# A decoder step in retention and cross attention: the samples' q and k rows reach all partitions by DMA through DRAM, not by selector products

## The chip, the cores and the metric

The kernel runs on one core of one Trainium2 chip. The metric is the device time of one execution in microseconds, the median of several runs. The work is float32 throughout; products of large matrices are made from two float32r halves of each operand (a high part `wh`, `B[0]`, `A[0]` and a low part `wl`, `B[1]`, `A[1]`), three products for one.

## The reference, cut to what matters

Two layers, each `x += mixer(norm(x)); x += cross_attention(norm(x)); x += conv_ffn(norm(x))`, for a prompt of 256 positions and for 8 samples of one new position each, with the same weights. Layer 0 mixes by retention; the change touches only the samples in it:

```python
q, k, v, g = jnp.split(h @ w_in, [nqk, 2 * nqk, 2 * nqk + nv], axis=-1)
q = rotary(q.reshape(B, L, RET_HEADS, RET_DK).astype(F32), offset)
k = rotary(k.reshape(B, L, RET_HEADS, RET_DK).astype(F32), offset) * (RET_DK ** -0.5)
...
o = att(q, k, v) + jnp.einsum('bihd,bhde->bihe', q * q_dec, s)   # reads the state
s = s * chunk_dec + jnp.einsum('bjhd,bjhe->bhde', k * k_dec, v)  # writes the new state
```

With one position a sample needs, for each of 4 heads, its old state (256 x 512) times its q row, and the new state, gamma times the old one plus the outer product of its k row and its v row.

## The kernel before

**Main stream.** `run` goes through a list of units in order. A unit is a tile of 128 output features: its weights come in chunks of 128 x 1024 (512 KB) into one of 6 raw slots (`wraw`), are split by ACT into `wh` and by DVE into `wl` (4 slots each), and TensorE makes three products of 264 columns for each step of 128 rows of the contraction (8 steps to a chunk). The order of the weights: retention in (48 chunks, with the prompt's memory keys and values of layer 0 among them), retention out (`ret_w_out`, 16 chunks, of which 9 come before `K.ret_done`), cross attention, FFN, then layer 1 in the same way.

**Everything else** is a task, a Python generator that issues some instructions and yields. `Clock` is a rough model of the engines' queues, the DMA among them; the task whose due time comes first goes next, and prefetches start when the model's DMA is not too far ahead and when the arena `ar` has room (`prefetch`, `reserve`). So the order of all instructions on all engines is fixed when the program is built, and any change of a cost, a wait or of the arena's size moves it. All loads and stores are issued by one queue, SP's, in order; DVE, ACT and TensorE are queues in order too.

**The samples of a head.** A state lies as 128 partitions x 4 x 256, the 256 of the head's q or k dimension along the free axis. So the q row must be there on every partition. `ret_qk` transposes q and k of the 8 samples to rows, and writes each as two float32r halves (partitions 0 to 7 and 32 to 39) into `rget` storage in `f` (q) and into `kst` (k). `bcast` then multiplies a column of the selector `sel` (40 partitions, given to TensorE 128 times over) by these 40 rows: two products of 256 columns put two samples' rows on all partitions of a PSUM bank. `settle` copies the bank to SBUF (128 x 512, ACT). `ret_samples` uses that for four `scalar_tensor_tensor` with `accum_out` for each state (`junkt<-kvt,x`), `ret_update`, which runs beside the two FFNs, for four `scalar_tensor_tensor` that make the new state (`kvt<-x,vst,kvt`). A pair of rows serves two states; there are 16 pairs for q and 16 for k.

**After the samples** of a head come `ret_norm` (a norm over the head's output of prompt and samples: products with a column of ones, Newton steps on DVE, three small products that spread the factors, an ACT copy, two DVE products of 128 x 528) and `ret_fin`, which makes the head's four tiles of `B`: for each a DVE product, an ACT cast for the high half, a DVE subtraction for the low half. `K.ret_done` holds the main stream until that is done for all four heads; the tenth chunk of `ret_w_out` is the first that reads tiles 12 to 15 of `B`, head 3's.

Of the kernel before, what the change touches and what calls it, by code (L numbers as in the profile page):

```python
# [56 lines left out]
C_ID, C_ONE, C_COS, C_SIN, C_MASK = 0, P, 2 * P, 2 * P + NT, 2 * P + 3 * NT  # L57
C_DEC = C_MASK + H * T
C_SEL = C_DEC + 2 * H
C_SUM = C_SEL + S  # L60
# [7 lines left out]
def _constants():  # L68
    half = D // H // 2
    inv = np.float32(10000.0) ** (-np.arange(half, dtype=np.float32) / np.float32(half))  # L70
    pos = np.concatenate([np.arange(T), np.full(S, PAST)]).astype(np.float32)
    ang = (inv[:, None] * pos[None, :]).astype(np.float32).astype(np.float64)
    c = np.zeros((P, NCST), np.float64)
    c[:, C_ID:C_ID + P] = np.eye(P)
    c[:, C_ONE:C_ONE + P] = 1.0
    c[:, C_COS:C_COS + NT] = np.cos(ang)
    c[:, C_SIN:C_SIN + NT] = np.sin(ang)
    c[:, C_SIN + NT:C_SIN + 2 * NT] = np.cos(ang)
    j = np.arange(P)[:, None]
    i = np.arange(T)[None, :]  # L80
    for h in range(H):
        rel = i - j
        m = np.where(rel >= 0, _gamma(h) ** np.maximum(rel, 0), 0.0) / 16.0
        c[:, C_MASK + h * T:C_MASK + (h + 1) * T] = m
        for t in range(2):
            c[:, C_DEC + 2 * h + t] = _gamma(h) ** (T - 1 - t * P - np.arange(P)) / 16.0
    for s in range(S):
        c[[s, LO + s], C_SEL + s] = 1.0
        c[LO * (s % 4) + s, C_SUM + s] = 1.0
    return c.astype(np.float32)  # L90
# [80 lines left out]
class Clock:  # L171
    """A rough model of the engines' queues, by which the order of the instructions is chosen."""
# [79 lines left out]
class Kern:  # L252
# [188 lines left out]
    def split_at(self):  # L441
        """When the next chunk of the stream can be split, as far as that is known."""
# [7 lines left out]
    def calm(self, n):  # L450
        """When chunk n of the stream, which is not the next to be used, may get in the way of other work."""
# [28 lines left out]
    def need(self, c):  # L480
        """Chunk c is the next of the stream to be used."""
# [164 lines left out]
    def proj(self, src, src_rhs, evac, n=NT, parts=False, tag=None):  # L646
        """The chunks in src hold the rows of one 128-feature tile, in order; with parts a unit each."""
# [31 lines left out]
    def pair(a, b, cut=6):  # L679
        """Two projections of one chunk each, with the last rows of the contraction of both at the end."""  # L680
# [24 lines left out]
    def newton(self, a, y, n, root=False):  # L705
        """y = a ** -0.5: a first guess from the exponent bits, or the root from a table, then Newton steps."""
# [14 lines left out]
    def rsqrt_mean(self, sq, n, cnt, wide=False, tok=None, root=False):  # L721
        """[128, n] copies of (column sums of sq / cnt + EPS) ** -0.5; a generator that returns them."""
# [42 lines left out]
    def norm_later(self, wide=False):  # L765
        """The factors of the norm over what self.sq holds, as self.r, a few steps on."""
# [190 lines left out]
    def ret_qk(self, h):  # L957
# [37 lines left out]
    def rget(self, n):  # L995
        b = self.rarena.get(n)
        while b is None:
            yield WAIT
            b = self.rarena.get(n)
        return b  # L1000
# [73 lines left out]
    def ret_samples(self, h):  # L1074
        hd = self.hd[h]
        while "qk" not in hd["flags"]:
            yield WAIT
        yield from self.lock("s")
        qr = hd["qr"].ap
        acc = self.get(4 * S)  # L1080
        av = acc.v(4, S)
        nb = yield from self.bcast(qr, 0)
        yield WAIT
        nxt = yield from self.settle(nb)
        for pr in range(4):
            cur = nxt
            if pr < 3:
                nb = yield from self.bcast(qr, 2 * pr + 2)
            else:
                hd["qr"].free()  # L1090
# [10 lines left out]
            if pr < 3:  # L1101
                nxt = yield from self.settle(nb)
# [18 lines left out]
    def ret_update(self, heads):  # L1121
        """New retention states of the samples: gamma * state + k v^T."""
# [3 lines left out]
        nb = yield from self.bcast(self.kst[:, order[0][0], :], order[0][1])  # L1126
        t0 = self.now
        for n, (h, s) in enumerate(order):
            if s % 2 == 0:
                yield WAIT  # L1130
# [72 lines left out]
    def residual(self, gain, scale=False):  # L1203
        """What becomes of the sums of output tile m: they are added to x."""
# [49 lines left out]
    def blocks(self, plan, rows, evac):  # L1254
        """A unit for each (chunk, tiles, k): the chunk holds rows k, ... of the contraction for some output tiles."""
# [60 lines left out]
    def parts(self, src, dims):  # L1316
        """A copy of src in two parts of fewer bits that add up to it."""
# [74 lines left out]
    def bcast(self, src, n0):  # L1392
        """Two rows of src, n0 and n0 + 1, on all partitions of a bank."""
        b = yield from self.wbank()
        for s2 in range(2):
            self.mm(self.ps[:, b, s2 * 256:(s2 + 1) * 256], self.sel[:, n0 + s2:n0 + s2 + 1].to_broadcast([LO + S, P]),
                    src[:LO + S, :256], True, True)
        return b
# [25 lines left out]
    def gather(self, b, rows):  # L1424
        """Column s of half t of bank b: row 32 (s % 4) + s of columns 128 t to 128 t + 127 of rows."""
# [136 lines left out]
    def lru_prep(self):  # L1562
        # 8 log_sigmoid(lam) = 8 (min(lam, 0) - log1p(exp(-|lam|))), log1p(z) = 2 artanh(z / (2 + z))
# [22 lines left out]
    def lru(self):  # L1586
# [3 lines left out]
        def half(name, m, n=4):  # L1590
            """Feature tile m of a buffer that is kept for half of the tiles."""
# [154 lines left out]
# How eager each part of the program is, in us: patience (2), slack of the task kinds 1 to 3, tilt, ahead.  # L1746
# [7 lines left out]
def tile_hybrid_step(ctx: ExitStack, tc: tile.TileContext, ins, outs):  # L1754
# [12 lines left out]
    K.sel = pool.tile([LO + S, S], F32R, name="sel")  # L1767
# [14 lines left out]
    K.kst = pool.tile([P, H, 256], F32R, name="kst")  # L1782
# [7 lines left out]
    nc.vector.memset(kvt[:, 0, :1024], 0.0)  # L1790
    nc.vector.tensor_copy(K.kst.rearrange("p a b -> p (a b)"), kvt[:, 0, :1024])
# [3 lines left out]
    ROOM = 28160 + 1024 * (6 - K.NR) - 128 - 128 - S - 2 * 2 * KD * M  # L1795

    def enter(nb, maxpre, reserve, slots, main):
        def go():
# [11 lines left out]
            if nb == 16:  # L1810
                K.rarena = Arena(ft, 512)
                nc.vector.tensor_copy(ft[:, :512], kvt[:, 0, :512])
# [88 lines left out]
    def staged(units, n):  # L1901
        """The last part of each of the first n tiles comes after the other parts of all of them."""
# [6 lines left out]
    items += [tune(12, 7200, (1,), 4), lambda: K.cp(K.sel, K.cst[:LO + S, C_SEL:C_SEL + S]),  # L1909
              lambda: K.add(K.mem_norm(0), 1)] + qkv[0][6:]  # L1910
# [3 lines left out]
    def out(w, plan, rows, gain):  # L1914
        """plan: what to wait for, or chunks of w."""
# [132 lines left out]
```

## Time and profile before

| | |
|---|---|
| median of 3 runs | 1046.58 us (1046.05 to 1047.74) |
| span of the profiled execution, first to last instruction | 1044.7 us |
| what the median of the runs has beyond that span | 1.9 us |
| TensorE busy | 1023.0 us (98%) |
| VectorE (DVE) busy | 807.4 us (77%) |
| ScalarE (ACT) busy | 589.4 us (56%) |
| DMA, mean | 245 GB/s |

The profiled execution's own time is its span; no other time of it is shown, so the rest of a run is taken as 1.9 us throughout. Times in the rows are us from the span's start. A matmul's duration covers its way through the array, and the next starts before it ends, so what a product costs a full TensorE is read from the starts of the rows, not from durations. In a merged row of several instructions the time runs from the first start to the last end.

### The profile page before, as it was taken

The numbers are of one execution on the slowest core, as the hardware profiler recorded it, in microseconds if no ns is written. First come the engines' busy times: TensorE is split into PE (matmuls) and PEld (weight loads), VectorE is DVE, ScalarE is ACT, GpSimd is POOL, SyncE is SP. The second block draws the span as 40 slices with busy tenths as digits, with TensorE's granted clock in tenths as the row PEclk, the third lists the DMA queues.
The fourth block names the chain that finished last, engine by engine and source line by source line (L and its number), as shares of the span: only waits on it lengthen the run. The fifth ranks groups of instructions, "written<-read, shape, count | busy, mean of one in ns | idle before, by whom it ended". The sixth has DMA issues, their size and how long they took to land.

```text
span 1044.7 us, 20974 instructions
## 1 busy us (share of the span) xinstructions
PE 1023.0 (98%) x8158; PEld 966.4 (93%) x8158; DVE 807.4 (77%) x1685; ACT 589.4 (56%) x979; POOL 84.4 (8%) x190
## 2 busy tenths in 40 slices
PE   7999999999999999999999999999999999999996
PEld 7988999889998868999999999999878999999996
DVE  7968788777677644898988776989755898898773
ACT  6554555455545434575676554697444666766552
POOL 0000000000000000023221000400000222121000
PEclk9999999999999999999999999999999999999998
DMA  9667766774766897567888977546886668777851
GB/s 371 207 216 248 272 224 232 263 262 164 271 218 235 297 315 256 191 212 259 266 297 291 301 235 233 172 164 233 311 286 223 209 203 290 272 256 272 299 192 62
DMA packets 70916, 255.45 MB, mean 245 GB/s; under 512 B 8096, under 2 KB 8736, under 8 KB 70304
## 3 DMA queue, kind: packets, MB, share of 16 engines
q1 hardware_dynamic: 70384, 253.53, 70.4%
q8 instruction: 64, 1.05, 0.4%
q10 hardware_dynamic: 432, 0.58, 0.2%
q14 instruction: 36, 0.29, 0.1%
HBM read 229.34 MB, written 24.74 MB: 243 GB/s over the span
## 4 chain that ended last, share of the span: by engine, by line
PE 87%; DVE 6%; DMA 3%; ACT 3%; issue 1%; SPq 0%; DVEq 0%; ACTq 0%
PE ps L274 83%; PE ps L279 3%; DVE wl L293 2%; DVE x L299 2%; DVE x L293 1%; DMA kvt<-in_cache_v 1%; DMA x<-in_cache_k 1%; ACT x L329 1%; PE ps L289 1%; ACT L329 1%; ACT wh L333 1%; DMA kvt<-in_cache_k 1%; DVE x L318 0%; DMA wraw<-in_ret_w_in 0%; DVE B L293 0%
## 5 line engine op out<-in xcount | busy, mean ns | idle before, releaser
L274 PE MATMUL ps<-A,wh 128*128 128x264 f32 x2816 | 525.1, 287 | 7.1 <-ACT A L329 6.3
L333 ACT CAST wh<-wraw 128x1024 fp32r<-128x1024 f32 x284 | 297.2, 1049 | 281.3 <-PE ps L274 237.2
L274 PEld LDWEIGHTS ps<-A,wh 128*128 128x128 f32 x2816 | 437.2, 189 | 16.0 <-ACT A L329 6.3
L293 DVE TENSOR_TENSOR wl<-wraw,wh 128x1024 fp32r<-128x1024 f32 x296 | 359.2, 1220 | 93.4 <-ACT wh L333 85.6
L274 PE MATMUL ps<-A,wl 128*128 128x264 f32 x1408 | 400.1, 284 | 0.1
L274 PE MATMUL ps<-B,wh 128*128 128x264 f32 (+1 forms) x1664 | 311.8, 288 | 2.2 <-DVE B L293 2.2
L274 PEld LDWEIGHTS ps<-B,wh 128*128 128x128 f32 x1664 | 257.3, 188 | 12.7 <-issue 8.6
L274 PEld LDWEIGHTS ps<-A,wl 128*128 128x128 f32 x1408 | 265.1, 188 | 0.4 <-DVE wl L293 0.3
L274 PE MATMUL ps<-B,wl 128*128 128x264 f32 (+1 forms) x832 | 235.5, 283 | 0.0
L274 PEld LDWEIGHTS ps<-B,wl 128*128 128x128 f32 x832 | 156.2, 188 | 0.0
L293 DVE TENSOR_TENSOR x<-ps,x 128x264 f32<-128x264 f32 (+2 forms) x248 | 83.9, 364 | 33.1 <-PE ps L274 21.2
L337 POOL COPY x<-x 128x16 f32<-128x16 f32 (+2 forms) x162 | 78.3, 518 | 268.1 <-DVE x L293 217.2
L329 ACT ACTIVATE x<-x 128x264 f32<-128x264 f32 (+4 forms) x166 | 59.7, 389 | 20.2 <-DVE x L293 8.7
L299 DVE SCALAR_TENSOR_TENSOR x<-x,par 128x280 f32<-128x280 f32 (+3 forms) x128 | 61.5, 488 | 2.3
L333 ACT COPY x<-ps 128x512 f32<-128x512 f32 (+3 forms) x85 | 39.2, 475 | 42.0 <-PE ps L274 31.2
L299 DVE SCALAR_TENSOR_TENSOR kvt<-x,vst,kvt 128x256 f32<-128x256 f32 x128 | 53.3, 477 | 1.3 <-ACT kvt L329 1.3
L299 DVE SCALAR_TENSOR_TENSOR junkt<-kvt,x 128x256 bf16<-128x256 f32 x128 | 46.4, 420 | 9.1 <-DMA kvt<-in_state_ret 6.4
L293 DVE TENSOR_TENSOR x<-x 128x264 f32<-128x264 f32 (+6 forms) x106 | 44.8, 435 | 7.7 <-ACT x L329 5.8
L333 ACT CAST B<-x 128x264 fp32r<-128x264 f32 (+2 forms) x84 | 34.7, 417 | 24.5 <-DVE x L293 17.4
L329 ACT ACTIVATE x<-x,par 128x280 f32<-128x280 f32 (+2 forms) x64 | 38.6, 605 | 8.9 <-DVE x L293 5.9
L293 DVE TENSOR_TENSOR B<-x,B 128x264 fp32r<-128x264 f32 (+2 forms) x84 | 36.7, 438 | 8.4 <-ACT B L333 8.2
L274 PE MATMUL ps<-wh,B 128*128 128x512 f32 x128 | 42.5, 400 | 0.0
(100 smaller groups left out, 703.6 us busy)
## 6 DMA issues: line engine op xcount, KB each, us to landing
wraw<-in_ffn_w_up SPq DMA_DIRECT2D x96, 512.0 KB, 4.4
kvt<-in_state_ret SPq DMA_DIRECT2D x64, 512.0 KB, 6.0
wraw<-in_ret_w_in SPq DMA_DIRECT2D x48, 512.0 KB, 4.4
wraw<-in_ffn_w_down SPq DMA_DIRECT2D x48, 512.0 KB, 4.7
out_ret_s<-kvt SPq DMA_DIRECT2D x32, 512.0 KB, 5.1
x<-in_cache_v SPq DMA_DIRECT2D x18, 512.0 KB, 6.7
wraw<-in_xa_w_k SPq DMA_DIRECT2D x16, 512.0 KB, 4.4
wraw<-in_xa_w_v SPq DMA_DIRECT2D x16, 512.0 KB, 4.1
```

The lines of the kernel that those rows point to most:

```text
L274: self.last = self.nc.tensor.matmul(out, lhsT, rhs, start=start, stop=stop)
L279: self.nc.tensor.matmul(out, lhsT, rhs, start=start, stop=stop, tile_position=(0, LO * j))
L289: self.nc.tensor.transpose(out, in_, self.ident[:n, :n])
L293: self.nc.vector.tensor_tensor(out=out, in0=a, in1=b, op=op)
L299: self.nc.vector.scalar_tensor_tensor(out, a, s, b, op0, op1, **kw)
L329: self.nc.scalar.activation(out, in_, func, **kw)
L333: self.nc.scalar.copy(out, in_)
L337: self.nc.gpsimd.tensor_copy(out, in_)
```

## The change

q and k rows no longer go through TensorE and PSUM to all partitions. `ret_qk` writes plain float32 rows of q and k side by side into one buffer of 8 partitions, `ret_rows` stores it into a DRAM tile `qk` (4 heads x 2 x 8 samples x 256), and `spread` loads two samples' rows (2 KB) from there into each of 128 partitions. `bcast`, `settle`, `rget`, `sel`, `kst` and the two zero fills at the start are gone; the 1024 words of `kst` go to the arena (`ROOM`). The samples of a head wait for a flag `rows` that the model sets 1 us after the store. Comments are gone too.

```diff
-        hr = yield from self.rget(256)
-        hd["qr"] = hr
-        hv, kv = hr.ap, self.kst[:, h, :]
-        self.cp(hv[:S, :], ps[:S, :256])
-        self.act(kv[:S, :], ps[:S, 256:], AF.Copy, scale=1.0 / 16.0)
-        self.tt(hv[LO:LO + S, :], ps[:S, :256], hv[:S, :].bitcast(F32), SUB)
-        self.stt(kv[LO:LO + S, :], ps[:S, 256:], 1.0 / 16.0, kv[:S, :].bitcast(F32), MUL, SUB)
+        rows = yield from self.wget(512)
+        rv = rows.ap[:S, :512]
+        self.cp(rv[:, :256], ps[:S, :256])
+        self.act(rv[:, 256:], ps[:S, 256:], AF.Copy, scale=1.0 / 16.0)
+        self.add(self.ret_rows(h, rows))
...
+    def ret_rows(self, h, rows):
+        yield self.c.written(rows.ap[:, :512])
+        t = self.store(self.qk[h].rearrange("t s d -> s t d"), rows.ap[:S, :512].rearrange("s (t d) -> s t d", t=2))
+        yield t + 1000.0
+        rows.free()
+        self.hd[h]["flags"].add("rows")
+
+    def spread(self, h, t, s):
+        b = yield from self.wget(512)
+        while self.c.used(b.ap) > self.now + 500.0:
+            yield self.c.used(b.ap) - 400.0
+        src = self.qk[h, t, s:s + 2, :].rearrange("s d -> (s d)").partition_broadcast(P)
+        return b, self.load(b.ap[:, :512], src)
...
     def ret_samples(self, h):
-        while "qk" not in hd["flags"]:
+        while "rows" not in hd["flags"]:
             yield WAIT
...
-        nb = yield from self.bcast(qr, 0)
-        yield WAIT
-        nxt = yield from self.settle(nb)
+        nxt = yield from self.spread(h, 0, 0)
         for pr in range(4):
-            cur = nxt
+            cur, at = nxt
             if pr < 3:
-                nb = yield from self.bcast(qr, 2 * pr + 2)
-            else:
-                hd["qr"].free()
+                nxt = yield from self.spread(h, 0, 2 * pr + 2)
+            if at > self.now:
+                yield at
...
     def ret_update(self, heads):
-        nb = yield from self.bcast(self.kst[:, order[0][0], :], order[0][1])
+        nxt = yield from self.spread(*order[0][:1], 1, 0)
...
             if s % 2 == 0:
-                yield WAIT
-                kb = yield from self.settle(nb)
+                kb, at = nxt
+                if at > self.now:
+                    yield at
                 if n + 2 < len(order):
-                    nb = yield from self.bcast(self.kst[:, order[n + 2][0], :], order[n + 2][1])
+                    nxt = yield from self.spread(order[n + 2][0], 1, order[n + 2][1])
...
-    def bcast(self, src, n0):
-        b = yield from self.wbank()
-        for s2 in range(2):
-            self.mm(self.ps[:, b, s2 * 256:(s2 + 1) * 256], self.sel[:, n0 + s2:n0 + s2 + 1].to_broadcast([LO + S, P]),
-                    src[:LO + S, :256], True, True)
-        return b
-
-    def settle(self, b):
-        t = yield from self.wget(512)
-        self.cp(t.ap[:, :512], self.ps[:, b, :])
-        self.unbank(b)
-        return t
...
-    ROOM = 28160 + 1024 * (6 - K.NR) - 128 - 128 - S - 2 * 2 * KD * M
+    ROOM = 29184 + 1024 * (6 - K.NR) - 128 - 128 - S - 2 * 2 * KD * M
```

Counted over the whole program: TensorE loses the 64 selector products and nothing else; ACT loses 32 copies of 128 x 512; DVE loses 8 operations on 8 x 256 and three fills at the start; SP issues 4 stores and 32 loads more. The rest is the same work in another order. Three places show the order.

On TensorE, at the start of the update of the states beside the first FFN (`kst,sel` are the selector products), before:

```order
L274 MATMUL ps<-A,wh 128x264 x2
L274 MATMUL ps<-A,wl 128x264
L274 MATMUL ps<-kst,sel 128x256 x2
L274 MATMUL ps<-A,wh 128x264 x2
L274 MATMUL ps<-A,wl 128x264
L274 MATMUL ps<-kst,sel 128x256 x2
```

With the change, the same place:

```order
L272 MATMUL ps<-A,wh 128x264 x2
L272 MATMUL ps<-A,wl 128x264
L272 MATMUL ps<-A,wh 128x264 x2
L272 MATMUL ps<-A,wl 128x264
L272 MATMUL ps<-sq,cst 128x264
L272 MATMUL ps<-A,wh 128x264 x2
```

The pairs are gone and the main stream's products stand next to each other; `sq,cst` is the norm's product, which stands a few steps later in the program before.

On DVE, the end of head 3's norm and its four tiles of `B` (`x<-x 128x264`, then `B<-x,B`), then the weights (`wl`) up to the first sums of the output projection (`x<-ps,x`, the tenth chunk's result), before:

```order
L293 TENSOR_TENSOR x_88<-x_88 128x264
L293 TENSOR_TENSOR B_85<-x_88,B_85 128x264
L293 TENSOR_TENSOR x_88<-x_88 128x264
L293 TENSOR_TENSOR B_85<-x_88,B_85 128x264
L293 TENSOR_TENSOR wl<-wraw,wh 128x1024 x9
L293 TENSOR_TENSOR x<-ps,x 128x264 x2
```

With the change, on DVE:

```order
L291 TENSOR_TENSOR wl<-wraw,wh 128x1024 x2
L291 TENSOR_TENSOR x_86<-x_86 128x528 x2
L291 TENSOR_TENSOR x_86<-x_86 128x264
L291 TENSOR_TENSOR B_84<-x_86,B_84 128x264
L291 TENSOR_TENSOR x_86<-x_86 128x264
L291 TENSOR_TENSOR B_84<-x_86,B_84 128x264
L291 TENSOR_TENSOR x_86<-x_86 128x264
L291 TENSOR_TENSOR B_84<-x_86,B_84 128x264
L291 TENSOR_TENSOR x_86<-x_86 128x264
L291 TENSOR_TENSOR B_84<-x_86,B_84 128x264
L291 TENSOR_TENSOR wl<-wraw,wh 128x1024
L291 TENSOR_TENSOR x<-ps,x 128x264 x2
```

And on TensorE with the change, from the three small products that spread head 3's factors to the tenth chunk, whose products wait for that head's tiles one after the other:

```order
L272 MATMUL ps<-cst,x_86 128x128 [waits DVE_49]
L272 MATMUL ps<-cst,x_86 128x128
L272 MATMUL ps<-cst,x_86 128x8
...
L272 MATMUL ps<-B_84,wh 128x264 x2
L272 MATMUL ps<-B_84,wl 128x264
L272 MATMUL ps<-B_84,wh 128x264 [waits Activation_49]
L272 MATMUL ps<-B_84,wh 128x264 [waits DVE_49]
L272 MATMUL ps<-B_84,wl 128x264
L272 MATMUL ps<-B_84,wh 128x264 [waits Activation_49]
L272 MATMUL ps<-B_84,wh 128x264 [waits DVE_49]
L272 MATMUL ps<-B_84,wl 128x264
```

Five steps of the main stream stand between the small products and the first of these waits (eight rows left out). Head 3's samples moved back by some 100 steps of the main stream: before, nine chunks of weights were split between its last tile and the sums, now one is.

On SP, the loads around the end of layer 0's cross attention (`in_cache_v` are the samples' memory values), before:

```order
L350 DMA wraw<-in_xa_w_o 128x1024
L350 DMA x_88<-in_cache_v 128x1024
L350 DMA wraw<-in_xa_w_o 128x1024 x2
L350 DMA x_88<-in_cache_v 128x1024 x3
L350 DMA wraw<-in_xa_w_o 128x1024
L350 DMA x_88<-in_cache_v 128x1024
L350 DMA wraw<-in_xa_w_o 128x1024 x2
```

With the change:

```order
L348 DMA x_86<-in_cache_v 128x1024
L348 DMA wraw<-in_xa_w_v 128x1024
L348 DMA x_86<-in_cache_v 128x1024 x4
L348 DMA wraw<-in_xa_w_v 128x1024
L348 DMA x_86<-in_cache_v 128x1024 x3
L348 DMA wraw<-in_xa_w_o 128x1024 x2
```

The last of these loads moved from behind the sixth of the eight `xa_w_o` chunks to ahead of the first.

## Rows read from the trace of the kernel before

**Rows 1.** The page: span, and busy time of the engines.

```profile
span 1044.7 us, 20974 instructions
PE 1023.0 (98%) x8158; PEld 966.4 (93%) x8158; DVE 807.4 (77%) x1685; ACT 589.4 (56%) x979; POOL 84.4 (8%) x190
```

**Rows 2.** Windows beside the first FFN: busy us of each engine, clock, DMA.

```profile
440.00:460.00 20.00, 19.86 (x161) 19.37 (x160) 19.79 (x39) 15.07 (x24) 5.91 (x11) 1.00 0.56 178
500.00:520.00 20.00, 20.00 (x164) 19.72 (x164) 19.16 (x38) 13.69 (x23) 6.52 (x12) 1.00 0.80 258
```

**Rows 3.** Timeline of PE: start, us, then the products; a selector pair.

```profile
431.69 0.28 PE L274 MATMUL ps<-A,wl 128*128 128x264 f32 x1
...
432.06 0.28 PE L274 MATMUL ps<-A,wl 128*128 128x264 f32 x1
432.27 0.50 PE L274 MATMUL ps<-kst,sel 40*128 40x256 f32 x2
432.69 0.51 PE L274 MATMUL ps<-A,wh 128*128 128x264 f32 x2
433.04 0.28 PE L274 MATMUL ps<-A,wl 128*128 128x264 f32 x1
```

**Rows 4.** Timeline of PE: a pair next to other small products.

```profile
92.16 0.50 PE L274 MATMUL ps<-f,sel 40*128 40x256 f32 x2
92.59 0.83 PE L274 MATMUL ps<-cst,x 128*128 128x1 f32 x6
```

**Rows 5.** Groups by form: what is removed.

```profile
L333 ACT COPY x<-ps 128x512 f32<-128x512 f32 x48 | 27.6, 582 | 17.6 <-PE ps L274 13.8 <-DVE junkt L299 3.0 <-ACT kvt L333 0.5
...
L274 PE MATMUL ps<-f,sel 40*128 40x256 f32 x32 | 8.0, 329 | 0.0
L274 PE MATMUL ps<-kst,sel 40*128 40x256 f32 x32 | 8.0, 329 | 0.0
```

**Rows 6.** Timeline of all engines: head 3's norm, first tiles of `B`.

```profile
235.74 0.51 PE L274 MATMUL ps<-cst,x 128*128 128x128 f32 x4
...
236.28 0.38 ACT L333 COPY x<-ps 128x264 f32<-128x264 f32 x1 [1.05 <-PE ps L274]
...
236.69 1.32 DVE L293 TENSOR_TENSOR x<-x 128x528 f32<-128x528 f32 x2
...
239.98 0.43 DVE L293 TENSOR_TENSOR x<-x 128x264 f32<-128x264 f32 x1
240.44 0.41 ACT L333 CAST B<-x 128x264 fp32r<-128x264 f32 x1 [1.31 <-DVE x L293]
240.88 0.43 DVE L293 TENSOR_TENSOR B<-x,B 128x264 fp32r<-128x264 f32 x1 [0.48 <-ACT B L333]
241.24 0.42 DVE L293 TENSOR_TENSOR x<-x 128x264 f32<-128x264 f32 x1
```

**Rows 7.** Timeline: the output projection starts on PE; head 3's last tile.

```profile
249.23 0.40 PE L274 MATMUL ps<-B,wh 128*128 128x264 f32 x2
...
256.26 0.43 DVE L293 TENSOR_TENSOR B<-x,B 128x264 fp32r<-128x264 f32 x1 [0.49 <-ACT B L333]
```

**Rows 8.** Windows, columns as in rows 2: where TensorE has gaps.

```profile
368.00:372.00 4.00, 3.46 (x30) 2.85 (x28) 2.75 (x7) 0.76 (x2) 0.00 (x0) 1.00 0.95 246
372.00:376.00 4.00, 3.16 (x29) 2.52 (x30) 0.56 (x1) 1.40 (x3) 0.00 (x0) 1.00 0.89 348
712.00:716.00 4.00, 2.70 (x23) 2.49 (x21) 3.97 (x6) 1.84 (x3) 0.90 (x2) 1.00 0.54 177
...
1036.00:1040.00 4.00, 1.45 (x6) 1.35 (x6) 1.98 (x6) 0.38 (x1) 0.00 (x0) 0.50 0.02 7
```

**Rows 9.** DMA issues: count, KB each, median us from issue to landing.

```profile
kvt<-in_state_ret SPq DMA_DIRECT2D x64, 512.0 KB, 6.0
...
out_ret_p<-x SPq DMA_DIRECT2D x8, 256.0 KB, 5.8
```

**Rows 10.** Waits: engine, tile, line, released by; us in total, times, longest.

```profile
DVE junkt L299 <- DMA kvt<-in_state_ret: 6.4, 4, 3.3
...
SPq L350 <- DVE wl L293: 516.7, 196, 10.8
```

More of the change, by code (lines that the diff above doesn't have):

```diff
@@ L58 @@
 C_DEC = C_MASK + H * T
-C_SEL = C_DEC + 2 * H
-C_SUM = C_SEL + S
+C_SUM = C_DEC + 2 * H
 NCST = C_SUM + S
@@ L87, in _constants @@
     for s in range(S):
-        c[[s, LO + s], C_SEL + s] = 1.0
         c[LO * (s % 4) + s, C_SUM + s] = 1.0
@@ L993, in ret_qk @@
         hd["flags"].add("qk")
-    def rget(self, n):
-        b = self.rarena.get(n)
-        while b is None:
-            yield WAIT
-            b = self.rarena.get(n)
-        return b
+    def ret_rows(self, h, rows):
[10 more added lines that the diff above has]
+        return b, self.load(b.ap[:, :512], src)
     def ret_attn(self, h):
@@ L1075, in ret_samples @@
         hd = self.hd[h]
-        while "qk" not in hd["flags"]:
+        while "rows" not in hd["flags"]:
             yield WAIT
         yield from self.lock("s")
-        qr = hd["qr"].ap
         acc = self.get(4 * S)
         av = acc.v(4, S)
-        nb = yield from self.bcast(qr, 0)
-        yield WAIT
-        nxt = yield from self.settle(nb)
+        nxt = yield from self.spread(h, 0, 0)
         for pr in range(4):
-            cur = nxt
+            cur, at = nxt
             if pr < 3:
-                nb = yield from self.bcast(qr, 2 * pr + 2)
-            else:
-                hd["qr"].free()
+                nxt = yield from self.spread(h, 0, 2 * pr + 2)
+            if at > self.now:
+                yield at
             for s2 in range(2):
@@ L1100, in ret_samples @@
             cur.free()
-            if pr < 3:
-                nxt = yield from self.settle(nb)
         while "attn" not in hd["flags"]:
@@ L1129, in ret_update @@
             if s % 2 == 0:
-                yield WAIT
-                kb = yield from self.settle(nb)
+                kb, at = nxt
+                if at > self.now:
+                    yield at
                 if n + 2 < len(order):
-                    nb = yield from self.bcast(self.kst[:, order[n + 2][0], :], order[n + 2][1])
+                    nxt = yield from self.spread(order[n + 2][0], 1, order[n + 2][1])
             st = yield from self.take(("up", h, s))
@@ L1390, in xa_prompt @@
         xh["flags"].add("prompt")
-    def bcast(self, src, n0):
-        b = yield from self.wbank()
-        for s2 in range(2):
-            self.mm(self.ps[:, b, s2 * 256:(s2 + 1) * 256], self.sel[:, n0 + s2:n0 + s2 + 1].to_broadcast([LO + S, P]),
-                    src[:LO + S, :256], True, True)
-        return b
-    def settle(self, b):
-        t = yield from self.wget(512)
-        self.cp(t.ap[:, :512], self.ps[:, b, :])
-        self.unbank(b)
-        return t
     def samples(self, b, w, kind, l, h):
@@ L1766, in tile_hybrid_step @@
     K.par = pool.tile([P, NPRM], F32, name="par")
-    K.sel = pool.tile([LO + S, S], F32R, name="sel")
+    K.qk = ctx.enter_context(tc.tile_pool(name="rows", bufs=1, space=bass.MemoryType.DRAM)).tile([H, 2, S, 256], F32, name="qk")
     K.junkt = pool.tile([P, 2, 256], BF16, name="junkt")
@@ L1781, in tile_hybrid_step @@
     K.rfree, K.hfree = deque(range(K.NR)), deque(range(K.NH))
-    K.kst = pool.tile([P, H, 256], F32R, name="kst")
     K.vst = pool.tile([P, H, 4, S], F32, name="vst")
@@ L1789, in tile_hybrid_step @@
     K.r0 = None
-    nc.vector.memset(kvt[:, 0, :1024], 0.0)
-    nc.vector.tensor_copy(K.kst.rearrange("p a b -> p (a b)"), kvt[:, 0, :1024])
     box = []
     FR = 3072
-    ROOM = 28160 + 1024 * (6 - K.NR) - 128 - 128 - S - 2 * 2 * KD * M
+    ROOM = 29184 + 1024 * (6 - K.NR) - 128 - 128 - S - 2 * 2 * KD * M
     def enter(nb, maxpre, reserve, slots, main):
@@ L1810, in go @@
             if nb == 16:
-                K.rarena = Arena(ft, 512)
-                nc.vector.tensor_copy(ft[:, :512], kvt[:, 0, :512])
                 K.mn = (bt[:, 0, 8:, :M], bt[:, 1, 8:, :M])
@@ L1908, in tile_hybrid_step @@
     items = [policy(0), enter(16, 0, 7200, (1,), 7), start, K.pair(*qkv[0][:2], 4), want_mem] + qkv[0][2:6]
-    items += [tune(12, 7200, (1,), 4), lambda: K.cp(K.sel, K.cst[:LO + S, C_SEL:C_SEL + S]),
-              lambda: K.add(K.mem_norm(0), 1)] + qkv[0][6:]
+    items += [tune(12, 7200, (1,), 4), lambda: K.add(K.mem_norm(0), 1)] + qkv[0][6:]
     items += qkv[1] + [K.mem_sure(0)] + kv0[:4] + qkv[2] + kv0[4:6] + gs[0] + qkv[3] + kv0[6:8] + gs[1] + kv0[8:] + gs[2] + gs[3]
```

## The prediction

> **What bounds the kernel now.** I read the page first: TensorE is busy 1023.0 of 1044.7 us [rows 1], so what it issues sets the time, and the question for each edit is whether it takes products from TensorE or makes it wait. The windows over the span then show where it is full. Beside the first FFN it issues 164 products in 20 us without a gap; in the window where DVE is fullest (19.79 of 20) TensorE already misses 0.14 us [rows 2]. Gaps of any size are few: 0.54 and 0.84 us in cross attention with the DMA engines 89 to 95% busy, 1.30 us in the recurrent layer with DVE full [rows 8]. The timeline gives what a product costs a full TensorE. A step of the main stream (three products of 264 columns) runs from 431.69 to 432.06, so 0.37 us; the next step has a selector pair in it and runs from 432.06 to 433.04, so 0.98 us [rows 3].
>
> **What the change takes from TensorE.** 32 pairs of selector products. The page's 329 ns mean [rows 5] is a passage through the array, not a cost; the cost is the starts: 0.98 - 0.37 = 0.61 us for a pair in the main stream [rows 3]. Only 0.42 us of it lies between the pair and what follows; the rest is delay ahead of the pair and behind it. Of the 32 pairs in the timeline 25 stand so, alone between main products; 7 touch other small products, which would break the stream anyway, and for those I take 0.43 us [rows 4]. Sum: 25 x 0.61 + 7 x 0.43 = 15.3 + 3.0 = 18.3 us, 16 pairs in retention and 16 beside the FFNs. Bounds: 32 x 0.43 = 13.8 and 32 x 0.61 = 19.5 us.
>
> The Trainium skill, page "TensorE: Matmul & The Clock Gate", section "Back-to-back issue gap", prices a product of N columns alone at N / 2.4 + 2.5 ns when warm, so 109 ns for 256 columns, and by that figure the pairs would give 64 x 0.109 = 7.0 us, 11.3 us less than the rows. The trace does not agree for these products: the start-to-start time of a pair is 0.43, not 0.22 us [rows 4], and I go by the rows.
>
> **What it takes from the others.** 32 ACT copies of 0.58 us, 18.6 us [rows 5], and 3 us of small DVE work. ACT is at 56% and DVE at 77% [rows 1], and TensorE hardly waits for them, so I cost this at nothing. The three fills at the start lie ahead of the first weights: nothing.
>
> **What it adds.** SP issues 36 more transfers, 8 MB in all. SP's queue spends half the span waiting for a raw slot, which DVE's `wl` frees [rows 10], so issuing is free. Landing is not shown for such a load. The nearest rows: a store with the same 2 KB per partition takes 5.8 us, a state of twice the size 6.0 us [rows 9]. A head's samples now wait for two landings one after the other, some 12 us, where they waited for two products and a copy. That is no time in itself, since the main stream goes on; it counts only where the samples' end holds the stream.
>
> **Where it counts: the tenth chunk of the output projection.** Before, the projection starts at 249.23 and head 3's last tile is there at 256.26 + 0.43 = 256.7 [rows 7]; the tenth chunk starts 72 steps in, at 249.23 + 72 x 0.37 = 275.9, so 19 us of cover. With the change the order puts the small products that spread head 3's factors five steps ahead of that chunk: the cover is gone. I put the rows of before into the new order. Small products end at 235.74 + 0.51 = 236.25, five steps take 1.85, so TensorE reaches the first wait at 238.1. ACT's copy and DVE's two products of 128 x 528 end at 236.69 + 1.32 = 238.01; then come the four tiles, with nothing between them now. From a tile's start (239.98) its high half is there after 0.87 us, its low half after 1.33, and the next tile starts after 1.26 [rows 6]. The last low half is there at 238.01 + 3 x 1.26 + 1.33 = 243.1, and two products later, at 243.4, TensorE is through what it would have done by 238.1 + 4 x 0.37 = 239.6. That is a stall of 3.8 us; two splits of weights now stand ahead of the norm on DVE, and I take 4.0. Bounds: 0, if head 3 runs earlier than the planned order needs, and 7: in the stall TensorE works about a third of the time, and at 1.45 busy of 4 us the granted clock stood at 0.50, at 2.70 of 4 it stayed at 1.00 [rows 8]; at half clock for some 3 us the next steps would cost 3 us more. Nothing gives the stall back: behind it the stream is full again.
>
> **The rest of the new order.** In layer 0's cross attention the 32 loads of the samples' memory end ahead of the output weights, six chunks (17 us of stream) earlier than before. The DMA engines there are 89 to 95% busy already, and the gaps in TensorE are 1.4 us [rows 8]. Bounds: 1.4 us gained, if these gaps go; 9 us lost, if six loads of 524 KB at the 348 GB/s of that window, 1.5 us each, have to be waited for in full. I take 1.0 lost, near the rows: the same nearly full DMA costs 1.4 now. In retention DVE stands 6.4 us in four waits for states [rows 10] and TensorE has no gap there, since up to four chunks lie split ahead of it. With 16 loads of q rows on the same engine I take 1.0 us lost; the bounds are 0 and the rival below. Beside the FFNs a pair of rows is loaded two states, about 20 us, ahead: nothing.
>
> **Sum:** 1044.7 - 18.3 + 4.0 + 1.0 + 1.0 = 1032.4 us of span; with the 1.9 us that the median has beyond the span, 1034.3 us.
>
> **Rivals.**
> (a) *The stall is covered.* Head 3's samples run ahead of the plan, or ahead of the waiting products by 4 us. For it: the order is only an order, an instruction may start as soon as its inputs are there. Against: the small products are themselves in TensorE's queue, five steps ahead of the chunk. Then 1034.3 - 4.0 - 1.0 = 1029.3 us with a quiet retention.
> (b) *Transfers hold cross attention.* All 9 us of the bound: 1034.3 + 8 = 1042.3 us. For it: 95% busy DMA. Against: the bytes of the stage stay the same.
> (c) *Slower: DVE waits for q rows.* A `junkt` operation on DVE now waits for a load that was issued only one chunk of weights (2.9 us) earlier, if it lands as late as rows 9 say; behind it on DVE stand the `wl` splits, and TensorE waits for those. The longest such wait now is 3.3 us [rows 10], and it is covered. If of each of the 16 loads 2.0 us reached TensorE, that is 32 us in place of the 1.0 taken: 1065 us. It decides from 14.3 / 16 = 0.9 us for each. Against: the four split chunks are 11 us of cover.
> (d) *No change.* Two ways. The fixed part of a pair's cost stays, because DVE's splits set the pace as soon as TensorE runs freer: then a pair gives back only its stream time, 2 x 0.12 = 0.25 us (a third of a step for each product [rows 3]), 8 us in all, and 1034.3 + 10.3 = 1044.6 us. Or every stall at its bound. For it: DVE at 19.79 of 20 in one window [rows 2]. Against: over the span DVE has 237 us to spare [rows 1]. The Trainium skill's price above (same page and section) would lead to about the same time, 1045.6 us, and it has its chance within this case.
>
> On the loads of (c): the Trainium skill, page "DMA: Bandwidth & Descriptors", section "Rules for kernel authors", says that a broadcast as the outermost, short dimension confines a transfer to a few of the sixteen engines; here the outermost dimension is the 128 partitions, so by that rule all sixteen work and the load is like any other. No row shows it yet.
>
> **Chances.** The forecast 0.52, (a) 0.15, (b) 0.15, (c) 0.10, (d) 0.08. The time is that of the forecast, 1034.3, whose own range with its bounds is 1030 to 1039. The range takes in (a) and (b), from 1027 (the pairs at 19.5 us and no stall) to 1044, and leaves out (c) and (d), 0.18. A measurement of this kernel can't tell a change under 0.2% (2.1 us) from none. Faster by more: forecast, (a) and (b), 0.82; within: (d), 0.08; slower: (c), 0.10.
>
> **What the changed profile would show.** TensorE's products 64 fewer and its steps in the stretches beside the FFNs at 0.37 us without breaks; the stretches from 440 to 600 and from 820 to 1000 each about 5 us shorter. In the tenth chunk of the output projection a wait of TensorE for `B` from ACT and DVE, 3 to 5 us in four parts; if it isn't there, (a). In cross attention a wait for `in_cache_k` or `in_cache_v` of 1 to 3 us; of 5 or more, (b). In retention `junkt` waits for `x<-qk`, and TensorE stays full; if its gaps there sum to 5 us or more, (c). A landing of `x<-qk` of 4 to 7 us; far more, 20 us say, and the loads are held by the one row that they all read, which would make the prediction wrong, as would a main stream whose steps stay above 0.37 us with the pairs gone.

## The result, and the profile after

The changed kernel takes 1031.97 us (median of 4 runs, 1030.98 to 1032.11), the kernel before, on the same chip, 1046.48 us (4 runs). The ratio is 0.9847, with a 95% interval of 0.9832 to 0.9861: 1.5% or 14.5 us faster. The profiled spans are 1029.2 and 1044.7 us. One thing the count under the change leaves out: six casts of weights to their high half went from ACT (284 to 278) to DVE (12 to 18).

The page of the changed kernel, answering to [rows 1]: TensorE has 64 products and 17.0 us of work less.

```profile
span 1029.2 us, 20860 instructions
PE 1006.0 (98%) x8094; PEld 957.4 (93%) x8094; DVE 803.9 (78%) x1680; ACT 567.9 (55%) x940; POOL 83.9 (8%) x190
```

Both programs put the same 6912 products of the weight stream through TensorE in the same order. So the start of the k-th of them can be subtracted from its start before, and the difference of two such differences says what a stage gained. Worked out so from the two traces, and from those of the experiments below (us against the kernel before; minus is faster). The columns end at products 1400, 1830, 2500, 4300, 5200 and 6911; the first cut stands 13 steps ahead of the output projection, the others near the stages' ends.

```
                    retention  output   cross      FFN 0  recurrent layer,  FFN 1   sum
                               proj.    att. 0            cross att. 1
the change            -10.3    +8.1     -1.8       -5.2      -0.8           -5.0   -15.0
e1 first pair early    -9.3    +1.8     -2.2       -5.3      +0.9           -5.0   -19.2
e2 full rows           -3.6     0.0     -0.3       -3.2      -0.1           -2.9   -10.1
e3 update only         -0.5     0.0     -0.4       -5.3      +5.0           -5.0    -6.0
e4 pairs twice         +3.2     0.0     +0.8       +1.8      +0.6           +1.8    +8.6
e5 retention early    -10.7    +2.3     +0.5        0.0      +1.3            0.0    -6.2
e6 old room            -7.9    +1.8     +0.2       -5.3      +3.1           -5.0   -12.7
e7 loads twice        +11.0    +7.8     -1.1       -5.2      -0.6           -5.0    +7.3
e8 spare loads         -5.5    +7.6     -1.0       -5.2      +0.2           -5.0    -8.9
```

(Each row's sum has up to 0.4 us that arise ahead of the first product, and rounding. What lies behind the last product is in no column: it gives the span 0.5 us more in the change and 1.1 us more in e1 and e3.) In the rows of the change, e1, e5, e6, e7 and e8 three groups of head 3's small products stand behind product 1400 and not ahead of it. They move 1.8 us from the first column to the second, which is all that e1 and e6 show there. Of the change's +8.1, then, 6.3 us are a loss, and its retention gained 8.5 us and not 10.3.

Where the gain is. Windows of the changed kernel, answering to [rows 2], columns as there: the steps are unbroken, 167 and 168 products in 20 us.

```profile
440.00:460.00 20.00, 20.00 (x168) 20.00 (x167) 19.72 (x44) 14.72 (x25) 4.02 (x15) 1.00 0.66 217
500.00:520.00 20.00, 20.00 (x167) 20.00 (x167) 17.50 (x35) 13.87 (x24) 4.69 (x12) 1.00 0.78 268
```

Where it loses: the tenth chunk of the output projection. The timeline of TensorE, DVE and ACT there:

```profile
263.99 2.36 DVE L291 TENSOR_TENSOR wl<-wraw,wh 128x1024 fp32r<-128x1024 f32 x2
264.54 0.73 PE L272 MATMUL ps<-cst,x 128*128 128x128 f32 x6
265.30 0.38 ACT L331 COPY x<-ps 128x264 f32<-128x264 f32 x1 [0.68 <-PE ps L272]
266.26 1.67 DVE L291 TENSOR_TENSOR x<-x 128x528 f32<-128x528 f32 x3
...
266.92 0.28 PE L272 MATMUL ps<-B,wl 128*128 128x264 f32 x1
268.43 0.85 PE L272 MATMUL ps<-B,wh 128*128 128x264 f32 x2 [1.23 <-ACT B L331]
269.68 1.05 PE L272 MATMUL ps<-B,wh 128*128 128x264 f32 x2 [0.28 <-ACT B L331]
270.94 1.05 PE L272 MATMUL ps<-B,wh 128*128 128x264 f32 x2
272.18 0.43 DVE L291 TENSOR_TENSOR B<-x,B 128x264 fp32r<-128x264 f32 x1 [0.48 <-ACT B L331]
272.20 1.06 PE L272 MATMUL ps<-B,wh 128*128 128x264 f32 x2
273.27 0.64 PE L272 MATMUL ps<-B,wh 128*128 128x264 f32 x2
...
276.57 0.48 PE L272 MATMUL ps<-B,wh 128*128 128x264 f32 x2
```

Four steps start 1.26 us apart, at the pace of the tiles [rows 6], and not 0.365. Unhindered they would run from 267.04 to 268.50; the next step starts at 273.27: 4.8 us. Two things make it longer than the 3.8 us worked out ahead. DVE is still in two splits until 266.26, when ACT's copy has been there since 265.68 (0.6 us). And the fourth step's products pass slowly already (from the last low half, there at 272.18 + 0.43 = 272.61, to 273.27, 0.66 us in place of 0.3). Then the next five steps take 3.30 us in place of 1.82, 1.5 us more. The windows say why, by their third number from the end:

```profile
268.00:270.00 2.00, 1.21 (x4) 0.67 (x4) 1.11 (x3) 1.16 (x3) 0.00 (x0) 0.97 0.87 272
270.00:272.00 2.00, 1.96 (x6) 1.28 (x5) 1.22 (x4) 1.15 (x3) 0.00 (x0) 0.50 1.04 430
272.00:274.00 2.00, 2.00 (x8) 1.62 (x8) 1.82 (x3) 0.15 (x1) 0.00 (x0) 0.50 0.94 295
274.00:276.00 2.00, 2.00 (x11) 2.00 (x11) 0.09 (x1) 0.07 (x1) 0.00 (x0) 0.50 0.95 375
```

From 270 to 276 the granted clock is 0.50, the lower of its two levels. TensorE is shown nearly full in those windows, since the rows above give 1.05 us of busy time to two products that take 0.40 elsewhere: the counts (6, 8, 11, against 17 at full pace) tell of the stall, the busy time doesn't. 4.8 + 1.5 = 6.3 us, the loss in the table.

The transfers. Landings, and the waits on DVE that answer to [rows 10]:

```profile
x<-qk SPq DMA_DIRECT2D x32, 256.0 KB, 5.5
```

```profile
DVE junkt L297 <- DMA kvt<-in_state_ret: 8.8, 6, 3.6
...
DVE junkt L297 <- DMA x<-qk: 3.9, 1, 3.9
```

A load of q or k rows lands in 5.5 us (3.5 to 7.0), and only one of the 16 in retention is waited for at all.

### The profile page after: what moved, and what is told of

Same layout as the page of the kernel before. It is cut to its first block, busy times and chain, and to the rows that moved or that the text cites. A ratio compares the mean times of both kernels' runs of the same rounds, so it can differ in the third digit from the quotient of the medians.

```text
span 1029.2 us, 20860 instructions
## 1 busy us (share of the span) xinstructions
PE 1006.0 (98%) x8094; PEld 957.4 (93%) x8094; DVE 803.9 (78%) x1680; ACT 567.9 (55%) x940; POOL 83.9 (8%) x190
## 4 chain that ended last, share of the span: by engine, by line
PE 87%; DVE 5%; ACT 3%; DMA 3%; issue 1%; SPq 0%; DVEq 0%; ACTq 0%
PE ps L272 83%; PE ps L277 3%; DVE wl L291 2%; DVE x L291 1%; ACT x L327 1%; PE ps L287 1%; DVE x L297 1%; ACT L327 1%; DMA x<-in_cache_v 1%; DMA kvt<-in_state_ret 1%; DMA wraw<-in_lru_wg 1%; ACT wh L331 0%; DMA wraw<-in_lru_w_in 0%; DVE B L291 0%; DMA wraw<-in_ret_w_in 0%
## 5 line engine op out<-in xcount | busy, mean ns | idle before, releaser
L331 ACT CAST wh<-wraw 128x1024 fp32r<-128x1024 f32 x278 | 290.9, 1050 | 283.6 <-PE ps L272 229.0
L297 DVE SCALAR_TENSOR_TENSOR junkt<-kvt,x 128x256 bf16<-128x256 f32 x128 | 46.3, 419 | 15.3 <-DMA kvt<-in_state_ret 8.8
L331 ACT COPY x<-ps 128x264 f32<-128x264 f32 (+4 forms) x61 | 23.9, 405 | 39.5 <-PE ps L272 32.0
```

The costliest lines, as they stand in the source:

```text
L297: self.nc.vector.scalar_tensor_tensor(out, a, s, b, op0, op1, **kw)
L331: self.nc.scalar.copy(out, in_)
```

## The experiments

Each kernel was timed against the kernel before on its own chip, where that took 1047.6 us (e1 to e4), 1048.9 (e5 to e7) and 1047.7 (e8). The ratios are to be compared; where a time is carried over to the chip of the change, it is the ratio times 1046.48 us.

**e1, a head's first pair early.** In `ret_samples` of the changed kernel:

```
-        yield from self.lock("s")
-        acc = self.get(4 * S)
-        av = acc.v(4, S)
         nxt = yield from self.spread(h, 0, 0)
+        yield from self.lock("s")
+        acc = self.get(4 * S)
+        av = acc.v(4, S)
```

> The changed kernel, but a head's first pair of q rows is loaded ahead of the turn of its samples. In the order the three small products that spread head 3's factors then stand 22 steps (8 us) ahead of the tenth chunk of the output projection, where they stood 5 steps (1.9 us) ahead. Theory: TensorE's stall there with its half clock, 6.3 us by the starts of the same products in the two traces, was only this lateness, so it goes: 1032.0 - 6.3 = 1025.7 us, between 1025 and 1027. Rival (the lack of time is DVE's and the transfers', and the stall only shows it there): it comes back at another place, 1030 to 1032 us.

Measured: 1027.03 us, ratio 0.9803 (0.9787 to 0.9819), clear of the change's interval. The table has the stall gone: +1.8 in the output projection, the moved small products alone. Windows of e1, in which its tenth chunk starts, at 267.91:

```profile
264.00:268.00 4.00, 4.00 (x35) 4.00 (x34) 2.72 (x6) 2.92 (x5) 0.62 (x1) 1.00 0.14 55
268.00:272.00 4.00, 4.00 (x35) 4.00 (x34) 3.45 (x5) 2.10 (x3) 0.34 (x1) 1.00 0.65 233
```

No gap, and full clock. Of the 6.3 us, 4.2 stayed in the sum; in the new order the recurrent layer lost 1.7 and retention 1.0, and cross attention gained 0.4. The stall was lateness of head 3: with a head's first load issued ahead of its turn it is gone. This is the fastest version found, 20.6 us ahead of the kernel before.

**e2, selectors over all rows.** The kernel before, with this in `bcast` (and `K.sel` allotted and filled over 128 partitions, two more lines):

```
-            self.mm(self.ps[:, b, s2 * 256:(s2 + 1) * 256], self.sel[:, n0 + s2:n0 + s2 + 1].to_broadcast([LO + S, P]),
-                    src[:LO + S, :256], True, True)
+            self.mm(self.ps[:, b, s2 * 256:(s2 + 1) * 256], self.sel[:, n0 + s2:n0 + s2 + 1].to_broadcast([P, P]),
+                    src[:, :256], True, True)
```

> The kernel before, with the selector products over all 128 rows in place of 40 (the rows added are zero); order, copies and counts are as before. Theory A: a pair costs 0.61 us and not two streams of 0.11 us because weight loads do not overlap where the number of active rows changes; with 128 rows a pair costs some 0.23 us, and 32 x 0.38 = 12 us are gained: 1034 us. Theory B: any such pair between steps costs 0.61 us, whatever its rows: 1046.5 us.

Measured: 1036.56 us, ratio 0.9894 (0.9879 to 0.9908): theory A, with 10 to 11 of its 12 us. TensorE's timeline in e2, at the first pair beside the first FFN (the place of [rows 3]):

```profile
428.10 0.28 PE L274 MATMUL ps<-A,wl 128*128 128x264 f32 x1
428.22 0.40 PE L274 MATMUL ps<-kst,sel 128*128 128x256 f32 x2
428.45 0.41 PE L274 MATMUL ps<-A,wh 128*128 128x264 f32 x2
```

The pair takes 0.23 us from its start to the next step's, and the product ahead of it 0.12. Before, in [rows 3], it was 0.42 and 0.21, with the same columns and the same work around it. The pair's weight loads now start 0.12 us ahead of it, with the product before:

```profile
428.10 0.31 PEld L274 LDWEIGHTS ps<-kst,sel 128*128 128x128 f32 x2
```

Beside the two FFNs the gain is 6.1 us (3.2 + 2.9), 0.38 for each pair, theory A in full; with the 16 x 0.23 us that these pairs still cost it makes up 9.8 of the change's 10.2, so the copies and small operations that ACT and DVE lose count for next to nothing there. What is missing lies in one place of retention: TensorE waits 1.12 us for the first head's norm, and from 92.7 to 96.2 us the granted clock is 0.50, which costs some 1.5 us more.

```profile
90.94 0.80 PE L274 MATMUL ps<-cst,x 128*128 128x1 f32 x6 [1.12 <-DVE x L293]
```

**e3, only the state updates through DRAM.** The kernel before, with the changed kernel's `ret_update`, and `ret_rows` storing k alone:

```
+        t = self.store(self.qk[h, 1], rows.ap[:S, :256])
...
-        nb = yield from self.bcast(self.kst[:, order[0][0], :], order[0][1])
+        nxt = yield from self.spread(*order[0][:1], 1, 0)
```

> The kernel before, where only the k rows of the state updates go through DRAM; retention keeps its selector products. Theory: the 16 pairs beside the two FFNs give back 0.64 us each there and nothing else moves: 1046.5 - 10.2 = 1036.3 us, no stall in the output projection. Rival: the gain of the change came from the new order in retention and cross attention: 1042 us or more.

Measured: 1039.11 us, ratio 0.9923 (0.9906 to 0.9939): 8.1 us gained by the ratio (8.5 by the medians) and not 10.2. The two FFNs gave their 10.3 us as expected; 5.0 us were lost in the recurrent layer, which the edit doesn't touch. One step there carries 3.8 of them. ACT and TensorE in e3:

```profile
680.58 0.85 ACT L329 ACTIVATE x<-ps,par 128x264 f32<-128x264 f32 x2
681.45 1.28 ACT L329 ACT_TABLE_LOAD   x1
682.75 1.08 ACT L329 ACTIVATE x<-x 128x1056 f32<-128x1056 f32 x1
683.85 1.28 ACT L329 ACT_TABLE_LOAD   x1
685.14 2.34 ACT L329 ACTIVATE x<-ps,par 128x264 f32<-128x264 f32 x6
685.67 0.51 PE L274 MATMUL ps<-A,wh 128*128 128x264 f32 x2 [1.62 <-ACT x L329]
```

ACT empties two of TensorE's banks, changes its function table twice for one other operation, and only then empties the next six, for which TensorE waits. Before, four were emptied ahead of that operation, and TensorE wasn't held there:

```profile
684.13 1.59 ACT L329 ACTIVATE x<-ps,par 128x264 f32<-128x264 f32 x4
```

This is the planner's order; TensorE's wait in this step is for ACT and not for a transfer.

**e4, each pair twice.** The kernel before, each selector product issued a second time into the same place, unknown to the planner:

```
+            self.nc.tensor.matmul(self.ps[:, b, s2 * 256:(s2 + 1) * 256], ..., start=True, stop=True)
             self.mm(self.ps[:, b, s2 * 256:(s2 + 1) * 256], self.sel[...].to_broadcast([LO + S, P]),
```

> The kernel before, each pair of selector products issued twice (the second overwrites the first's result with the same numbers). Theory by the rows (two more starts at 0.22 us each behind the first two): 32 x 0.43 = 13.8 us more, 1060.3 us. By streaming alone (0.11 us a product): 7.0 us more, 1053.5 us. If a pair's whole price of 0.61 us were paid again: 19.5 us more, 1066 us.

Measured: 1055.35 us, ratio 1.0079 (1.0060 to 1.0098), 8.3 us more by the ratio (7.7 by the medians): near streaming alone, and not the 0.22 us for each start that [rows 4] had suggested. TensorE's timeline in e4 (the products of L1396 are the added ones):

```profile
436.42 0.28 PE L274 MATMUL ps<-A,wl 128*128 128x264 f32 x1
436.63 0.38 PE L1396 MATMUL ps<-kst,sel 40*128 40x256 f32 x1
436.86 0.28 PE L274 MATMUL ps<-kst,sel 40*128 40x256 f32 x1
436.98 0.28 PE L1396 MATMUL ps<-kst,sel 40*128 40x256 f32 x1
437.09 0.27 PE L274 MATMUL ps<-kst,sel 40*128 40x256 f32 x1
437.29 0.51 PE L274 MATMUL ps<-A,wh 128*128 128x264 f32 x2
```

Starts are 0.21, 0.23, 0.12, 0.11, 0.20 us apart, and after the next product 0.23 again. Two long starts stand where the stream goes to 40 rows and two where it comes back; between them a product costs 0.12. The weight loads of the same stretch show it too:

```profile
436.31 0.19 PEld L274 LDWEIGHTS ps<-A,wl 128*128 128x128 f32 x1
436.63 0.18 PEld L1396 LDWEIGHTS ps<-kst,sel 40*128 40x128 f32 x1
436.74 0.18 PEld L274 LDWEIGHTS ps<-kst,sel 40*128 40x128 f32 x1
...
437.29 0.30 PEld L274 LDWEIGHTS ps<-A,wh 128*128 128x128 f32 x2
```

The load for `wl` at 436.31 stands 0.11 us ahead of its product at 436.42; the first load for `sel` starts with its product, at 436.63, the second again 0.12 us ahead of its own (436.74, 436.86), and the first load back at 128 rows starts with its product, at 437.29. So a pair's 0.61 us were 2 x 0.12 us of streaming and about 4 x 0.095 us of change of rows, paid once for a group, of two or of four. The other pairs bear it out: for the 25 that stand between main products, what a group takes out of the stream, with its delays ahead and behind, is 0.62 us in the mean before, 0.85 in e4 and 0.23 in e2.

**e5, only retention through DRAM.** The kernel before, with the changed `ret_samples` and e1's early first pair, and k's selector products kept:

```
+        t = self.store(self.qk[h, 0], rows.ap[:S, :256])
...
-        nb = yield from self.bcast(qr, 0)
+        nxt = yield from self.spread(h, 0, 0)
```

> The kernel before, where only the q rows go through DRAM (k keeps its selector products in the state updates), with a head's first pair loaded ahead of its turn as in the first run, so that no stall stands in the output projection. Theory: the 16 pairs of retention give back 0.6 us each and nothing else counts: 1046.5 - 9.7 = 1036.8 us. Rival (c) of the prediction in a mild form, each of the 16 loads holding DVE for 0.5 us: 1045 us.

Measured: 1042.34 us, ratio 0.9947 (0.9927 to 0.9967), 5.6 us gained; by the profiled spans 6.6. Retention with the projection gave 8.4 us (-10.7 + 2.3) and no stall; 1.8 us went in cross attention and the recurrent layer, which the edit doesn't touch either. Theory in the place, 3 to 4 us too hopeful in the sum (1040.9 us on the chip of the change).

**e6, the old room.** The changed kernel, with the planner's arena as before:

```
-    ROOM = 29184 + 1024 * (6 - K.NR) - 128 - 128 - S - 2 * 2 * KD * M
+    ROOM = 28160 + 1024 * (6 - K.NR) - 128 - 128 - S - 2 * 2 * KD * M
```

> The changed kernel with the planner's buffers as small as before (ROOM back to 28160; the 4 KB for each partition that the removed tile gave stay unused). No load is moved by hand; only the order that the planner finds differs, and in it head 3's last tile stands ahead of the tenth chunk. Theory (the stall is the order's, not the loads'): it goes, 1025 to 1028 us. Rival (two landings one after the other are what makes head 3 late): it stays, 1031 to 1033 us.

Measured: 1034.4 us, ratio 0.9869 (0.9849 to 0.9888): out of both ranges as it stands, and within the rival's when carried over to the chip of the change (1032.8 us). Still the stall is gone (+1.8 as in e1), without a load moved by hand, so it was the order's; the time alone would have misled. But the same edit lost 2.4 us in retention, 2.0 in cross attention and 3.9 in the recurrent layer against the change. 4 KB for each partition of the arena, with no instruction's work changed, move each of these stages by 2 to 4 us; whether by the order alone or by loads that start later for lack of room was not separated.

**e7, each load twice.** The changed kernel, in `spread`:

```
+        self.nc.sync.dma_start(out=b.ap[:, :512], in_=src)
         return b, self.load(b.ap[:, :512], src)
```

> The changed kernel, with each of the 32 loads of q or k rows issued twice into the same buffer; the order is that of the change. Theory: the loads lie ahead of their use, so 8.4 MB more cost nothing in retention and beside the FFNs; only head 3's, at the stall, are on the path and may add 1 to 3 us: 1032 to 1035 us. Rival (c): each load's landing reaches TensorE, and the 16 of retention add 1 us or more each: 1048 us or more.

Measured: 1054.92 us, ratio 1.0059 (1.0044 to 1.0074), 22 us behind the change, 21 of them in retention; beside the FFNs nothing. The size is the rival's, but the edit had put in a wait of its own. SP's issues in e7 (L1005 is the added load):

```profile
74.34 0.33 SPq L1005 DMA_DIRECT2D x<-qk  x1
82.46 0.33 SPq L348 DMA_DIRECT2D x<-qk  x1
82.84 0.43 SPq L348 DMA_DIRECT2D kvt<-in_state_ret  x1
83.78 0.32 SPq L1005 DMA_DIRECT2D x<-qk  x1
88.27 0.32 SPq L348 DMA_DIRECT2D x<-qk  x1
```

The second load writes where the first does and is held until that has landed, 8.1 and 4.5 us here, and behind it in SP's queue stand the states and weights. They come late, and the wait goes on to DVE and TensorE:

```profile
DVE junkt L297 <- DMA kvt<-in_state_ret: 34.2, 11, 5.6
```

```profile
100.02 0.59 PE L272 MATMUL ps<-A,wl 128*128 128x264 f32 x1 [3.45 <-DVE wl L291]
```

Part of the 21 us is the clock: from 99.7 to 113.4 us it is granted at 0.50. How much was not separated.

**e8, extra loads that nothing waits for.** The same number of extra transfers, each into one of eight spare buffers in DRAM:

```
+        self.nspare = (self.nspare + 1) % 8
+        self.nc.sync.dma_start(out=self.spare[self.nspare], in_=src)
         return b, self.load(b.ap[:, :512], src)
```

> The changed kernel, with each of the 32 loads of q or k rows accompanied by a second transfer of the same source to one of eight spare buffers in DRAM, issued just ahead of it. In the run before this one the second load went into the same buffer, so SP's queue stood until the first had landed (8.1 us the longest seen), and retention lost 21 us while the stretches beside the FFNs lost nothing. Here nothing has to land first; the order is that of the change. Theory (retention was held by SP's queue standing, not by the transfers' own time): little is lost, 1032 to 1036 us, and nothing beside the FFNs. Rival (256 KB more for each load is itself what DVE waits for): 1045 us or more.

Measured: 1037.58 us, ratio 0.9905 (0.9886 to 0.9924), 6.1 us behind the change where e7 was 22: theory, if 1.6 us above its range (0.5 when carried over to the chip of the change). Most of the loss, 4.3 us, lies in one place of retention, from 92 to 99 us: the first head's samples end at 90.3 us where they ended at 87.6, TensorE stands for 3.3 us instead of 0.55 ahead of the products of that head's norm, and the granted clock is 0.50 for 3.4 us behind it. DVE's waits for states grow from 8.8 to 15.3 us:

```profile
DVE junkt L297 <- DMA kvt<-in_state_ret: 15.3, 8, 3.2
```

```profile
95.31 0.80 PE L272 MATMUL ps<-cst,x 128*128 128x1 f32 x6 [3.29 <-ACT wh L331]
```

Whether the extra bytes or the extra places in SP's queue did it was not separated.

## Why the prediction came out right, and where it did not

The sign, the place of the gain and the place of the loss were right; three of the four terms were off by 1.9 to 2.8 us, one of them in its sign. That the time came out within 2.3 us of the forecast is partly luck: the stall cost 2.3 us more than was forecast, and against that the pairs gave 1.9 us more and cross attention 2.8. In us:

```
                                 predicted   measured in the stages
selector pairs                    -18.3     -10.2 (FFNs), about -10.0 (retention)
stall at the tenth chunk           +4.0      +6.3
cross attention, layer 0           +1.0      -1.8
waits in retention                 +1.0      +1.4
recurrent layer (not named)         0        -0.8
sum                               -12.3     -15.0
```

**The pairs.** The change in their start times was read rightly: 16 pairs beside the FFNs gave 10.2 us, 0.64 each, and 0.61 had been taken. In retention 8.5 us net are left; TensorE has 0.55 and 0.75 us of gaps in the windows 60 to 100 and 100 to 140 us, where it had none before, and 1.4 us more gaps in all of the first column, so the pairs there gave about 10.0. The starts before the change say the same: with the delay ahead and behind counted, six of the seven pairs that touch small products cost 0.62 to 0.68 us, one 0.55, and the 16 of retention 10.0. The prediction's 0.43 for them was the pair alone, without the delay around it; its upper bound of 19.5 us for all pairs was passed.

What failed is the reason behind the price. The prediction weighed the Trainium skill's 109 ns for a product of 256 columns (page "TensorE: Matmul & The Clock Gate", section "Back-to-back issue gap") against the row and said that the trace did not agree. e4 shows that it nearly does: 0.12 us for each product in an equal stretch. The rest of the pair's price was the change from 128 to 40 rows and back, which e2 takes away alone. The same page of the Trainium skill, section "Step-by-step: what each phase is for", says that a weight load is pulled ahead of running products when its row groups do not conflict or when it goes to the background buffer. In e4's rows a load runs ahead in a stretch of equal rows (by 0.11 us) and not at a change; which of the two conditions fails there they do not show. The Trainium skill's price as a forecast, 1045.6 us, failed because each pair stood between products of 128 rows and paid for the change twice, going in and coming back.

**The stall.** The mechanism and its four parts are as forecast; the term was too small. DVE's two splits added 0.6 us where 0.2 had been allowed. The half clock, put at 3 us in the upper bound and left out of the term, came and cost 1.5. 6.3 lies in the bounds of 0 to 7. e1 and e6 show that the stall was a matter of order; rival (a) did not come by itself.

**Cross attention.** The term had the wrong sign. The 0.54 and 0.84 us of gap in [rows 8] are one wait of 1.38 us, for a load of the samples' keys. With the change there is still one, for their values, but it is shorter. TensorE before:

```profile
372.84 0.84 PE L279 MATMUL ps<-x 128*32 128x256 f32 x10 [1.38 <-DMA x<-in_cache_k]
```

With the change:

```profile
375.30 1.06 PE L277 MATMUL ps<-x 128*32 128x256 f32 x12 [1.02 <-DMA x<-in_cache_v]
```

So the wait of 1 to 3 us that the prediction named is there, and the loads moved ahead of the output weights did not lengthen it; that step failed. Rival (b), 9 us of waits, is refuted. Over the stage TensorE's gaps shrank by 0.6 us only; the other 1.2 us of the gain must lie in how the small products stand among the steps, and no run took that apart. As e6 has +0.2 and e5 +0.5 there, it belongs to this order and not to the change as such.

**Retention and rival (c).** Landing at 5.5 us was in the forecast's 4 to 7, and one wait of 3.9 us is all that DVE shows for q rows. e7 shows that the mechanism of (c) is real where a transfer holds SP's queue, and e8 that 32 more transfers already cost 6.1 us, 4.3 of them in one tight place. "Issuing is free" was right beside the FFNs and too simple for retention.

**Rival (d)** fell with the windows at 168 and 167 products in 20 us: DVE, at 19.72 of 20 us, did not set the pace.

## What to carry to other kernels

Before moving small products off TensorE, look at their rows: a group with fewer rows than the stream around it paid 0.38 us for the change, and padding the selectors with zero rows, four lines, gave 10 of the 15 us that the whole change gave. When a value goes through DRAM, ask what its consumer is late for: here one head's late tiles held TensorE for 4.8 us in the new order, which with the half clock cost 6.3, and issuing each head's first load ahead of its turn gave 4.6 us back in the timed runs. Where a planner sets the order, compare stage by stage by the starts of equal products; a change of 1% in the sum can hide swings of 2 to 5 us in stages that it doesn't touch.

## What the runs showed of the hardware that was not expected

A weight load does not run ahead of the product before it where the number of active rows changes, here from 128 to 40 and back: four starts of 0.20 to 0.23 us in place of 0.12, two on the way in and two on the way out, the same for two products and for four. And in a stall of 4.8 us, in which TensorE did four steps, the granted clock fell to 0.50 (1.2 of 2.4 GHz) from 270 to 276 us: 1.5 us more, a third on top of the stall itself, and hidden in a row that shows the engine busy. Shorter waits did not all end alike: one of 1.1 us in e2 was followed by 3.4 us at 0.50, while in e6, with waits of 1.3 and 1.4 us in retention, the clock stayed at 1.00.
